# Hybrid encoder on one core: the low part of the far weight pages from a GpSimd subtraction instead of a negated copy and an accumulating DMA

## The chip, the core and the metric

The kernel runs on one core of a Trainium2 chip. The metric is the device time of one execution in microseconds; the kernel before takes 2670.23 us, the median of three runs (2668.58 to 2670.87). A core has TensorE (matmuls; PE in the profile, its weight loads PEld), VectorE (DVE), ScalarE (ACT), GpSimd (POOL) and SyncE (SP, which here only issues DMAs). Each engine works through its own queue in order; between engines only semaphores order the work. DMAs are issued from the queues of SyncE and GpSimd.

## What is computed

Two layers of a hybrid encoder on 256 tokens of width 4096, all in float32:

```python
h = rmsnorm(x, norm_w[l])
proj = h @ w_in[l]                       # 4096 x 11264
aq, ak, av, ag, rq, rk, rv, rg = jnp.split(proj, SPLIT_POINTS, axis=-1)
...                                      # rotary, grouped-query attention,
...                                      # bidirectional retention, gates
x = x + jnp.concatenate([a_out, r_out], axis=-1) @ w_out[l]   # 4096 x 4096
```

A final RMS norm follows. Nearly all of the work is the two products with `w_in` and `w_out`.

## The kernel before

**Three matmuls for one product.** TensorE multiplies in a float32 format with a shorter mantissa (fp32r). To keep float32 accuracy, each operand is split into a high part, rounded to fp32r, and a low part, the rest: `lo = x - hi`. A product is then three matmuls, hi·hi, lo·hi and hi·lo of weights and activations (lines 824 to 826). So every page of weights, 128 x 1024 float32 (512 KB), must be split on the core before TensorE can use it.

**How the weights are tiled.** A column block of 1024 outputs is worked through in 16 pairs of 256 rows, in four groups of four pairs. In the first pair of a group (`SEVEN`) a seven-product scheme in the manner of Strassen replaces eight products; it needs four pages (A, B and the sums T and U of raw pages, tiles `wsum`). Every other pair has two pages, A and B. There are 30 column blocks (11 for `w_in` and 4 for `w_out` in each of two layers) and 1200 pages; 960 of them are loaded as raw pages.

**Near and far pages.** 1082 pages are near. SyncE loads the raw page into one of five buffers (`wraw`, line 392), ScalarE casts it to the high part (`whi`), and VectorE subtracts (`wlo<-wraw,whi`); both parts stand in rings of five. The next load is issued when the low part has been put in its queue, and on the chip it waits for a free raw buffer.

The other 118 pages are far (`is_far`: page B of the pairs 2, 6, 10 and 14, but for the first two groups of the whole program). They go another way, past VectorE: `far_parts` has ScalarE cast the raw page to `fhi`, and ScalarE then writes the negated high part to `flo`; a DMA issued by GpSimd adds the same page of weights from HBM onto `flo`. So the raw buffer is free after the first copy, and its next load is issued at once, in `self.load()` at the end of `far_parts`. There is one buffer each for `fhi` and `flo`, and a far page is begun as soon as the far page before it is used up; it is used some ten pages later.

**What sets the order.** The program is written in a fixed order by a planner in Python. `ve` and `ac` wrap VectorE and ScalarE and add up an assumed cost for every operation (`ve.until`, `ac.until`); `now` is TensorE's planned time. Between products, `tick` puts in steps of other work (attention, retention, splitting of activations) where `room` finds that the parts of the coming pages will still be ready. Work for GpSimd's queue that belongs to far pages is kept in `self.adds` with the time from which it may be put in, and `add` puts it in when that time comes, or `take` does at the latest when the page is used:

```python
while self.adds and (now_all or self.adds[0][0] <= now.t + 0.5):
    self.adds.pop(0)[1]()
```

GpSimd's queue also holds the DMAs that store and fetch intermediate tiles (`store`, line 782, `fetch`, line 787, and the keys and values, line 1138) and the power in `rsqrt` (line 346). SyncE's queue holds the raw pages and some small tables and gains (`tables`, lines 318 and 321).

Of the kernel before, what the change touches and what calls it, by code (L numbers as in the profile page):

```python
# [13 lines left out]
AF = mybir.ActivationFunctionType  # L14
ALU = mybir.AluOpType
# [197 lines left out]
def hybrid_encoder(  # L213
# [15 lines left out]
    nc = tc.nc  # L229
    now = Now()  # L230
    ve, ac = Clock(nc.vector, vector_cost, now), Clock(nc.scalar, scalar_cost, now)
# [15 lines left out]
    def t(pool, shape, tag, bufs=None, dt=F32):  # L247
        kw = {} if bufs is None else {"bufs": bufs}
        return pool.tile(shape, dt, tag=tag, name=tag, **kw)

    def f32(v):
        return v.bitcast(F32)
# [99 lines left out]
    class Weights:  # L352
# [58 lines left out]
        def far_parts(self, g, src):  # L411

            g.hi = t(wp, [P, 2, NB], "fhi", FAR, F32R)
            g.lo = t(wp, [P, 2, NB], "flo", FAR, F32R)
            ac.copy(g.hi, src)
            ac.activation(g.lo, f32(g.hi), AF.Copy, scale=-1.0)
            g.high_at, g.low_at = ac.until, ac.until + FAR_LANDING
            self.adds.append((ac.until, partial(nc.gpsimd.dma_start, g.lo, g.src[0], accum_op=ALU.add)))
            self.load()

        def begin(self, g):

# [1142 lines left out]
```

## Time and profile before

| What | Value |
|---|---|
| three runs | 2670.87, 2670.23, 2668.58 us |
| profiled execution, span from first to last instruction | 2664.7 us |
| mean granted TensorE clock | 0.996 |
| DMA | 670.25 MB, mean 252 GB/s |
| far pages: negated copies on ScalarE | 118, 1062 ns each |
| far pages: accumulating DMAs | 86 for `w_in`, 32 for `w_out` |

The profile gives the span of its execution alone; the runs' times lie some 5.5 us above it.

How to read its lines. A group line names the source line, the engine, the operation, the tile written and the tiles read with their shapes, the count, the total busy time in us, the mean of one in ns, and then the idle time of the engine just before these instructions with what ended most of it. All of VectorE's and ScalarE's instructions carry line 198, that of the recording wrapper, so they are told apart by their tiles. A line of waits has the waiting instruction, what ended the wait, the sum in us, how often, and the longest. A line of the timeline has the start, the duration, the instruction, and in brackets the idle time before it with its releaser. SPq is SyncE's queue: its instructions only issue DMAs.

### The profile page before, as it was taken

The numbers are of one execution on the slowest core, as the hardware profiler recorded it, in microseconds if no ns is written. First come the engines' busy times: TensorE is split into PE (matmuls) and PEld (weight loads), VectorE is DVE, ScalarE is ACT, GpSimd is POOL, SyncE is SP. The second block draws the span as 40 slices with busy tenths as digits, with TensorE's granted clock in tenths as the row PEclk, the third lists the DMA queues.
The fourth block names the chain that finished last, engine by engine and source line by source line (L and its number), as shares of the span: only waits on it lengthen the run. The fifth ranks groups of instructions, "written<-read, shape, count | busy, mean of one in ns | idle before, by whom it ended". The sixth has DMA issues, their size and how long they took to land.

```text
span 2664.7 us, 33863 instructions
## 1 busy us (share of the span) xinstructions
PE 2621.3 (98%) x11832; PEld 2177.8 (82%) x11832; DVE 2079.2 (78%) x2579; ACT 1724.6 (65%) x2426; POOL 336.7 (13%) x478
## 2 busy tenths in 40 slices
PE   7999999999999999999999999999999999999997
PEld 5878888888888888888888888888888888888886
DVE  8877887887778797776978777887887688976765
ACT  7757676666555677555876666676565566865554
POOL 0011211111101110110111111211100011000000
PEclk9999999999999999999999999999999999999999
DMA  7888988887777787888888888988877787778885
GB/s 253 287 258 249 291 252 275 260 261 246 222 233 230 240 261 218 259 264 262 297 245 261 257 277 256 290 251 277 256 225 229 227 250 238 244 222 257 246 251 184
DMA packets 197660, 670.25 MB, mean 252 GB/s; under 512 B 23792, under 2 KB 30448, under 8 KB 197488
## 3 DMA queue, kind: packets, MB, share of 16 engines
q1 hardware_dynamic: 148912, 523.35, 57.2%
q0 software_dynamic: 48576, 144.73, 23.6%
q8 instruction: 92, 1.51, 0.2%
q14 instruction: 80, 0.66, 0.1%
HBM read 623.95 MB, written 44.04 MB: 251 GB/s over the span
## 4 chain that ended last, share of the span: by engine, by line
PE 92%; DVE 3%; DMA 3%; issue 1%; ACT 1%; POOL 0%; SPq 0%; POOLq 0%; DVEq 0%; ACTq 0%
PE M L825 30%; PE M L824 30%; PE M L826 30%; DVE wlo L198 1%; PE ps L825 1%; PE ps L826 1%; PE ps L824 1%; DMA wraw<-in_w_in 1%; DMA ca<-in_x 0%; DMA flo<-in_w_out 0%; DMA flo<-in_w_in 0%; ACT whi L198 0%; DMA tables<-in_k_norm 0%; DVE cb L198 0%; DVE x8l L198 0%
## 5 line engine op out<-in xcount | busy, mean ns | idle before, releaser
L198 ACT CAST whi<-wraw 128x1024 fp32r<-128x1024 f32 x842 | 820.7, 990 | 564.3 <-PE M L826 471.8
L198 DVE TENSOR_TENSOR wlo<-wraw,whi 128x1024 fp32r<-128x1024 f32 x842 | 950.4, 1143 | 272.5 <-ACT whi L198 261.0
L824 PE MATMUL M<-whi,x8h 128*128 128x512 f32 x1806 | 704.5, 390 | 0.4 <-DVE ca L198 0.3
L825 PE MATMUL M<-wlo,x8h 128*128 128x512 f32 x1806 | 704.0, 390 | 0.2 <-DVE wlo L198 0.2
L826 PE MATMUL M<-whi,x8l 128*128 128x512 f32 x1806 | 703.3, 389 | 0.0
L824 PEld LDWEIGHTS M<-whi,x8h 128*128 128x128 f32 x1806 | 339.9, 188 | 71.5 <-DVE ca L198 1.6
L826 PEld LDWEIGHTS M<-whi,x8l 128*128 128x128 f32 x1806 | 339.5, 188 | 71.0
L825 PEld LDWEIGHTS M<-wlo,x8h 128*128 128x128 f32 x1806 | 339.8, 188 | 70.1 <-DVE wlo L198 0.6
L198 ACT CAST whi<-wsum 128x1024 fp32r<-128x1024 f32 x240 | 252.6, 1053 | 180.2 <-PE M L826 161.2
L198 DVE TENSOR_TENSOR wlo<-wsum,whi 128x1024 fp32r<-128x1024 f32 x240 | 292.6, 1219 | 98.0 <-ACT whi L198 97.6
L825 PE MATMUL M<-wlo,x7h 128*128 128x512 f32 x840 | 327.5, 390 | 7.0 <-DVE wlo L198 7.0
L826 PE MATMUL M<-whi,x7l 128*128 128x512 f32 x840 | 327.5, 390 | 6.3 <-DVE x7l L198 6.3
L824 PE MATMUL M<-whi,x7h 128*128 128x512 f32 x840 | 327.1, 389 | 0.2 <-ACT whi L198 0.2
L824 PE MATMUL M<-whi,x 128*128 128x512 f32 x602 | 235.4, 391 | 9.2 <-ACT whi L198 9.2
L825 PE MATMUL M<-wlo,x 128*128 128x512 f32 x602 | 235.4, 391 | 1.2 <-DVE wlo L198 1.2
L826 PE MATMUL M<-whi,x 128*128 128x512 f32 x602 | 234.9, 390 | 0.0
L467 POOL DMA_DIRECT2D flo<-in_w_in x86 | 77.4, 900 | 1104.3 <-ACT flo L198 966.5
L198 DVE TENSOR_TENSOR wsum<-wraw 128x1024 f32<-128x1024 f32 x120 | 146.5, 1221 | 67.5 <-DMA wraw<-in_w_out 44.0
L198 ACT CAST fhi<-wraw 128x1024 fp32r<-128x1024 f32 x118 | 124.3, 1053 | 112.4 <-PE M L826 106.4
L826 PEld LDWEIGHTS M<-whi,x7l 128*128 128x128 f32 x840 | 157.9, 188 | 39.9 <-DVE x7l L198 7.1
L825 PEld LDWEIGHTS M<-wlo,x7h 128*128 128x128 f32 x840 | 157.8, 188 | 39.8 <-DVE wlo L198 7.8
L824 PEld LDWEIGHTS M<-whi,x7h 128*128 128x128 f32 x840 | 157.7, 188 | 32.7 <-ACT whi L198 0.7
(219 smaller groups left out, 3137.4 us busy)
## 6 DMA issues: line engine op xcount, KB each, us to landing
wraw<-in_w_in SPq DMA_DIRECT2D x703, 512.0 KB, 4.9
wraw<-in_w_out SPq DMA_DIRECT2D x256, 512.0 KB, 5.0
flo<-in_w_in POOLq DMA_DIRECT2D x86, 512.0 KB, 7.3
flo<-in_w_out POOLq DMA_DIRECT2D x32, 512.0 KB, 7.9
full<-next_dram POOLq DMA_DIRECT2D x18, 512.0 KB, 6.8
p_dram<-room POOLq DMA_DIRECT2D x64, 128.0 KB, 5.4
pT<-p_dram POOLq DMA_DIRECT2D x16, 512.0 KB, 5.9
next_dram<-room POOLq DMA_DIRECT2D x40, 128.0 KB, 5.7
```

The source lines that it names most:

```text
L198: return call(out, *args, **kwargs)
L467: self.adds.pop(0)[1]()
L824: nc.tensor.matmul(out, a[0], b[0], start=start, stop=False)
L825: nc.tensor.matmul(out, a[0], b[1], start=False, stop=False)
L826: nc.tensor.matmul(out, a[1], b[0], start=False, stop=stop)
```

## The change

In `far_parts` the negated copy and the accumulating DMA are gone. GpSimd subtracts the high part from the raw page instead, and the load that refills the raw buffer is put in behind the subtraction, since that reads the raw page.

```diff
             ac.copy(g.hi, src)
-            ac.activation(g.lo, f32(g.hi), AF.Copy, scale=-1.0)
             g.high_at, g.low_at = ac.until, ac.until + FAR_LANDING
-            self.adds.append((ac.until, partial(nc.gpsimd.dma_start, g.lo, g.src[0], accum_op=ALU.add)))
-            self.load()
+
+            def low():
+                nc.gpsimd.tensor_tensor(g.lo, src, f32(g.hi), op=ALU.subtract)
+                self.load()
+
+            self.adds.append((ac.until, low))
```

`FAR_LANDING`, the planner's allowance of 12 us until a far page's low part is there, stays.

## The prediction

> **What bounds the kernel now.** I read the page first, for the busy shares and the chain that ended last, and then the waits of the matmul engine.
>
> ```profile
> PE 2621.3 (98%) x11832; PEld 2177.8 (82%) x11832; DVE 2079.2 (78%) x2579; ACT 1724.6 (65%) x2426; POOL 336.7 (13%) x478
> PE 92%; DVE 3%; DMA 3%; issue 1%; ACT 1%; POOL 0%; SPq 0%; POOLq 0%; DVEq 0%; ACTq 0%
> ...
> PE M L824 <- ACT whi L198: 9.4, 3, 8.9
> PE M L825 <- DVE wlo L198: 8.5, 5, 5.6
> PE M L826 <- DVE x7l L198: 6.3, 2, 5.0
> PE M L825 <- DMA flo<-in_w_out: 1.2, 1, 1.2
> PE M L825 <- DMA flo<-in_w_in: 0.4, 1, 0.4
> ```
>
> TensorE is busy for 2621.3 of 2664.7 us. Its waits by name sum to 25.8 us, 8.9 of them the wait for the first page. Only 1.6 us (1.2 + 0.4) are waits for the low parts that the change makes in another way. So little can be won; the question is what the change takes away from the cover that keeps TensorE fed. That cover is made of VectorE and of the five raw pages:
>
> ```profile
> L198 DVE TENSOR_TENSOR wlo<-wraw,whi 128x1024 fp32r<-128x1024 f32 x842 | 950.4, 1143 | 272.5 <-ACT whi L198 261.0
> L198 DVE TENSOR_TENSOR wlo<-wsum,whi 128x1024 fp32r<-128x1024 f32 x240 | 292.6, 1219 | 98.0 <-ACT whi L198 97.6
> L198 DVE TENSOR_TENSOR wsum<-wraw 128x1024 f32<-128x1024 f32 x120 | 146.5, 1221 | 67.5 <-DMA wraw<-in_w_out 44.0
> ...
> L198 DVE TENSOR_TENSOR wsum<-wsum,wraw 128x512 f32<-128x512 f32 x120 | 83.1, 692 | 4.2
> L198 DVE TENSOR_TENSOR wsum<-wraw,wsum 128x512 f32<-128x512 f32 x120 | 82.0, 683 | 0.0
> ...
> L198 ACT ACTIVATE flo<-fhi 128x1024 fp32r<-128x1024 f32 x118 | 125.3, 1062 | 3.7
> L198 ACT CAST fhi<-wraw 128x1024 fp32r<-128x1024 f32 x118 | 124.3, 1053 | 112.4 <-PE M L826 106.4
> ...
> wraw<-in_w_in SPq DMA_DIRECT2D x703, 512.0 KB, 4.9
> wraw<-in_w_out SPq DMA_DIRECT2D x256, 512.0 KB, 5.0
> flo<-in_w_in POOLq DMA_DIRECT2D x86, 512.0 KB, 7.3
> ...
> SPq L392 <- DVE wlo L198: 1806.5, 667, 8.7
> SPq L392 <- ACT fhi L198: 119.6, 90, 4.4
> ```
>
> The near pages are 842 + 240 = 1082, one in 2664.7 / 1082 = 2.46 us. With a ring of five, a freed buffer is needed again four pages later, 9.9 us; less a cast (1.05, as `fhi`) and a subtraction (1.22), the low part stands ready 7.6 us early when nothing queues. The raw pages are 959 whole loads, one in 2.78 us; five slots turn round in 13.9 us, of which 4.9 are the transfer and 2.3 cast and subtraction, so a slot has 6.7 us to spare. The loads are one in-order queue on SyncE and wait for a slot nearly always: 1806.5 us for the subtraction that frees one, 119.6 us for the copy of a far page.
>
> **The change part by part.** *Removed from ScalarE*: 118 negated copies of 1062 ns, 125.3 us. ScalarE is 65% busy, so this is worth nothing except in the start. *Removed from the DMA*: 118 accumulating transfers of 512 KB, and TensorE's 1.6 us of waiting for them. I count −1.6.
>
> *Added to GpSimd*: 118 subtractions of 128x1024, each with two SBUF inputs. No row shows one. The only GpSimd arithmetic is the small power:
>
> ```profile
> L346 POOL TENSOR_TENSOR rst<-rst,half x16: 696/710/1615, 673.2 to 2356.2; 128x2 f32<-128x2 f32 x16
> ...
> 679.47 1.61 POOL L346 TENSOR_TENSOR rst<-rst,half 128x2 f32<-128x2 f32 x1 [5.56 <-DVE rst L198]
> ...
> 679.30 1.23 DVE L198 TENSOR_TENSOR wsum<-wraw 128x1024 f32<-128x1024 f32 x1
> 680.62 2.36 DVE L198 TENSOR_TENSOR wlo<-wraw,whi 128x1024 fp32r<-128x1024 f32 x2
> ```
>
> Its rate per element says nothing of a subtraction. I bound the price below by VectorE's same subtraction, 1.22 us, and above by the route replaced, 7.3 us from issue to landing. It is nearest to VectorE's row, one arithmetic step on the same shape; I take twice that, 2.4 us, as an estimate, since its smallest step above, on two elements, already takes 0.71 us. The Trainium skill, "GPSIMD Engine Reference", section 3.1, measures 4497 ns for an add of 2048 elements; half of that, an estimate of 2.25 us, would leave the sum as it is but for some tenths.
>
> *What it does to VectorE*: the power at 679.47 took 1.61 us where the median is 0.71. VectorE's operation with two SBUF inputs ran until 680.53; from there to the end at 681.08 are 0.55 us. So GpSimd stood still while VectorE read two tiles. That the reverse holds too (VectorE waits while GpSimd reads) this trace can't show, since two elements are read at once; from below it is no block at all, from above the whole 2.4 us. I take it as mutual. The Trainium skill, "SBUF — State Buffer", section "Who interferes with whom", says the same of a VectorE operation with two SBUF inputs against a GpSimd operation that reads SBUF: whichever is first keeps the other out for its whole length. This trace agrees in the one direction (1.61 against 0.71 us); with no block the sum below would lose its first term.
>
> The five VectorE rows above sum to 1554.6 us, 58% of the span. So a subtraction of 2.4 us costs VectorE 2.4 x 0.58 = 1.4 us on average, 164 us in all, and brings it from 78% to 84%. On average the 7.6 us lead hides that. Not where VectorE is full:
>
> ```profile
> 933.00:999.00 66.00, 66.00 (x303) 55.07 (x303) 60.24 (x96) 52.04 (x88) 6.76 (x10) 1.00 0.84 261
> 1266.00:1332.00 66.00, 64.83 (x287) 53.35 (x286) 62.56 (x118) 53.22 (x92) 10.47 (x17) 1.00 0.90 298
> 1399.00:1466.00 67.00, 67.00 (x297) 55.47 (x296) 58.93 (x88) 45.21 (x66) 11.13 (x14) 1.00 0.88 262
> 2265.00:2332.00 67.00, 67.00 (x302) 55.31 (x301) 63.95 (x99) 53.67 (x84) 3.70 (x5) 1.00 0.79 244
> ```
>
> The columns are PE, PEld, DVE, ACT and POOL busy. 118 pages in 2664.7 us are 2.9 in such a stretch, 4.1 us of block. VectorE has 5.8, 3.4, 8.1 and 3.1 us idle. If all of that idle could be used, the excess is 0.7 + 1.0 = 1.7 us; if none in the three fullest, 3 x 4.1 = 12.3. I take the middle, **+7**.
>
> *In the start* VectorE is on the path:
>
> ```profile
> 35.02 1.06 ACT L198 ACTIVATE flo<-fhi 128x1024 fp32r<-128x1024 f32 x1
> ...
> 37.64 1.23 DVE L198 TENSOR_TENSOR wlo<-wraw,whi 128x1024 fp32r<-128x1024 f32 x1 [0.68 <-ACT whi L198]
> ```
>
> Without the 1.06 us copy the cast behind it comes earlier, and VectorE loses its 0.68 us of idle; the first subtraction falls there and blocks 1.4 to 2.4 us. Net **+1.2** (0.7 to 1.7).
>
> *The moved load*: the load that refills a far page's slot is now issued behind the subtraction and waits for it on SyncE; behind it wait all later loads, and through them ScalarE's casts. Mostly it waits 2.4 us plus at most one VectorE operation, 1.2, inside the 6.7 us of a slot. But GpSimd's queue is in order too:
>
> ```profile
> POOL flo L467 <- ACT flo L198: 1427.9, 99, 47.6
> ...
> 861.14 1.06 ACT L198 ACTIVATE flo<-fhi 128x1024 fp32r<-128x1024 f32 x1
> ...
> 131.37 1.48 POOL L1138 DMA_DIRECT2D kv_dram<-vl  x2 [5.45 <-DVE vl L198]
> 132.84 0.94 POOL L467 DMA_DIRECT2D flo<-in_w_in  x1
> ...
> 868.54 0.89 POOL L1032 DMA_DIRECT2D rkq<-rq_dram  x1 [5.87 <-DMA rq_dram<-cb]
> 869.42 0.94 POOL L467 DMA_DIRECT2D flo<-in_w_in  x1
> ...
> 2178.83 0.94 POOL L467 DMA_DIRECT2D flo<-in_w_in  x1
> ...
> 133.27 0.59 SPq L318 DMA_DIRECT2D tables<-in_consts  x1
> ...
> 142.48 0.29 DVE L198 TENSOR_TENSOR C<-tables 128x128 f32<-128x128 f32 x1 [9.61 <-DMA tables<-in_k_norm]
> ```
>
> 99 of 118 times GpSimd was free and waited for ScalarE alone. At 869.42, and in the second layer at 2178.83, the far page stood behind a fetch that waited for its store. Until now that cost nothing but the low part's lateness: the slot was free at 861.1. Now it is held until 869.42 + 2.4 = 871.8, 10.7 us longer; that is 4.0 us more than the 6.7 to spare, partly under the 7.6 us lead of finished pages: 0 to 4 at each place, I take 2, together +4. At 132.84 the far page stands behind the stores of `vl`; SyncE's load then waits until 135.2, and the tables behind it, now issued at 133.27, go out 2.0 us later. VectorE idles 9.61 us for them, and TensorE's longest wait for `wlo` (5.6) is the same place: +1.5 (0 to 2), some of it returned by the missing transfer. Together **+5.5** (0 to 10).
>
> ScalarE's planned time is 1.05 us shorter for each far page, so some tasks move by a page; I count that at nothing, hidden by the lead of 7.6 us.
>
> The sum: +7 + 1.2 + 5.5 − 1.6 = +12.1, a span of 2676.8. The runs' median of 2670.23 lies 5.5 us over the profiled span; with that, **2682**.
>
> **The rivals.** *A, the cover holds*: the subtraction costs about 1.22 us, or VectorE isn't kept out. The block is then 0.7 us a page and 2.1 in a stretch, under the smallest idle of 3.1. The start nets nothing, the tables' +1.5 and the −1.6 cancel: 2670. For it speaks the 7.6 us lead; against it the 1.61 us of the power.
>
> *B, faster*: the transfers that are gone make the others land sooner.
>
> ```profile
> DMA packets 197660, 670.25 MB, mean 252 GB/s; under 512 B 23792, under 2 KB 30448, under 8 KB 197488
> ...
> DMA to landing us min/median/max: 4.4/6.4/8.9
> ```
>
> 118 x 0.524 MB are 62 of 670 MB, 9%. The tables that TensorE waits for land in up to 8.9 us; at the least, 4.4, that wait shrinks by 4.5. With −1.6 and −0.7 in the start: −6.8, 2663. Against it: everything that VectorE loses. It decides where the block is under some 0.5 us a page.
>
> *C, much slower*: the subtraction takes 4.9 us, four times VectorE's. The block is 2.8 us a page, 8.2 in a stretch; over the four idles above that is 12.5 (2.4 + 4.8 + 0.1 + 5.1) to 4 x 8.2 = 33, say 23. The start gives 3.5. The two late places hold 13.2 − 6.7 = 6.5 too long, half of it each, 6.5, and the tables 4.5. Less 1.6: +36, 2706. At the upper bound of 7.3 us VectorE loses 118 x 0.58 x 7.3 = 500 us (97% busy), and each slot is held 1.8 us over its spare (7.3 + 1.2 − 6.7), 212 in all: near 2890.
>
> **How the numbers follow.** The forecast has 0.44, its own range 2675 to 2695; A 0.20; B 0.14; C 0.16; its far end 0.06. About 0.2% (5.3 us) is what a measurement can tell from no change. Faster is B, 0.14; within is A and the forecast's lower edge, 0.22; slower 0.64. The range runs from 2664 to 2722: out are the far end, the upper part of C and half of B.
>
> **What would show it.** The subtraction's own duration on GpSimd (2.4; 1.2 for A, 4.9 for C), told by its spacing from what follows. VectorE's same subtractions longer than 1.22 us, or idle between them, beside it: 164 us in all. TensorE's waits for `wlo` up, most of it in 933 to 999, 1266 to 1332 and 2265 to 2332; its waits for `flo` gone. SyncE waiting some 9 us for GpSimd at about 862 and 2171, and the tables' wait near 140 longer than 5.6. Wrong it is if VectorE's operations keep their lengths beside the subtraction, or if TensorE's busy time itself grows.

## The result, and the profile after

The changed kernel takes 2684.59 us, the median of three runs (2684.30 to 2685.30), against 2670.23 before: +14.4 us, a ratio of 1.0055 with a 95% interval of 1.0035 to 1.0074. It is slower. The span of its profiled execution is 2683.5 us (2664.7 before).

The page of the kernel after: busy time by engine, the DMA total, the chain that ended last by engine, then one group of part 5 and two DMA issues of part 6.

```profile
PE 2630.1 (98%) x11832; PEld 2178.4 (81%) x11832; DVE 2190.9 (82%) x2579; ACT 1599.3 (60%) x2308; POOL 556.8 (21%) x478
...
DMA packets 180666, 608.36 MB, mean 227 GB/s; under 512 B 21904, under 2 KB 28560, under 8 KB 180496
...
PE 88%; DVE 7%; issue 2%; DMA 2%; ACT 1%; POOL 0%; SPq 0%; DVEq 0%; POOLq 0%; ACTq 0%
...
L419 POOL TENSOR_TENSOR flo<-wraw,fhi 128x1024 fp32r<-128x1024 f32 x118 | 325.0, 2755 | 1425.2 <-ACT fhi L198 1425.0
...
wraw<-in_w_in SPq DMA_DIRECT2D x703, 512.0 KB, 4.3
wraw<-in_w_out SPq DMA_DIRECT2D x256, 512.0 KB, 4.2
```

VectorE has the same 2579 instructions as before and is busy 111.7 us longer (2190.9 against 2079.2). The chain that ended last passes from TensorE (92% before, now 88%) to VectorE (3%, now 7%). What the change saves is there too, and buys nothing: ScalarE 125.3 us less, 62 MB less from HBM, pages that land in 4.3 us for 4.9. GpSimd is busy for 21% of the span, and of its 1425.2 us of idle time before the subtractions 1425.0 end with ScalarE's copy, so it is not the bound.

Groups of the kernel after, shapes kept apart; before, the first of them had a mean of 1219 ns, and the second is shown below it as it was:

```profile
L198 DVE TENSOR_TENSOR wlo<-wsum,whi 128x1024 fp32r<-128x1024 f32 x240 | 315.7, 1315 | 93.2 <-ACT whi L198 93.2
...
L198 DVE TENSOR_TENSOR cb<-cb,M 128x512 f32<-128x512 f32 x61 | 41.3, 679 | 0.8 <-PE M L829 0.7
```

```profile
L198 DVE TENSOR_TENSOR cb<-cb,M 128x512 f32<-128x512 f32 x61 | 41.4, 680 | 0.8 <-PE M L826 0.7
```

An operation with two inputs in SBUF has become longer; one that reads `M`, TensorE's output in PSUM, has kept its length (679 ns, 680 before). One place in the timeline shows why. The kernel after, GpSimd first, then VectorE (start, duration in us):

```profile
1460.86 2.95 POOL L419 TENSOR_TENSOR flo<-wraw,fhi 128x1024 fp32r<-128x1024 f32 x1
...
1460.34 1.22 DVE L198 TENSOR_TENSOR wlo<-wraw,whi 128x1024 fp32r<-128x1024 f32 x1
1461.48 3.41 DVE L198 TENSOR_TENSOR wlo<-wsum,whi 128x1024 fp32r<-128x1024 f32 x1
1464.81 0.75 DVE L198 TENSOR_TENSOR rot<-ca,S 128x256 f32<-128x256 f32 x2
...
1464.94 0.50 PE L828 MATMUL M<-wlo,x7h 128*128 128x512 f32 x1 [0.32 <-DVE wlo L198]
```

GpSimd's subtraction, issued at 1460.86, is 2.95 us long instead of 2.39, the shortest of the 118: it stood still until VectorE's first operation ended. VectorE's second operation is 3.41 us instead of 1.22: it stood still until GpSimd ended at 1463.81. TensorE took up this page's low part 0.05 us after it was done, and had waited 0.32 us. The same page before:

```profile
1446.00 1.22 DVE L198 TENSOR_TENSOR wlo<-wsum,whi 128x1024 fp32r<-128x1024 f32 x1
...
1450.48 0.39 PE L824 MATMUL M<-whi,x7h 128*128 128x512 f32 x1
```

It was done at 1447.22, and the matmul that reads it, the next after the one at 1450.48, came 3.49 us later. I call this time the lead of a page.

The waits of the kernel after, by engine: TensorE, SyncE, VectorE.

```profile
PE M L828 <- DVE wlo L198: 11.6, 16, 3.8
PE M L827 <- ACT whi L198: 10.9, 3, 9.8
PE M L829 <- DVE x7l L198: 7.6, 2, 7.1
PE M L827 <- DVE cb L198: 4.8, 3, 3.5
...
SPq L392 <- DVE wlo L198: 1532.3, 659, 8.9
SPq L392 <- POOL flo L419: 396.2, 109, 7.1
...
DVE C L198 <- DMA tables<-in_k_norm: 15.0, 2, 8.8
```

The waits for `flo` are gone; those for VectorE's tiles have grown from 15.1 us (8.5 + 6.3 + 0.3) to 25.0 (11.6 + 7.6 + 4.8 and 1.0 for `ca`). To see where TensorE loses time, slowed matmuls included, I set the start of each of its 11832 matmuls beside that of the matmul of the same number before. (In after 186 of them work on other tiles, since the planner moved some steps.) The table has how many us later it is, at some places given in the time of before. The kernels of experiments 9 (six blocks only), 11 (on VectorE) and 12 (VectorE, mixed) below stand beside it.

| at, us | after | six blocks only | on VectorE | VectorE, mixed |
|---|---|---|---|---|
| 9 (first matmul) | 0.95 | 0.11 | 0.06 | -0.16 |
| 60 | 2.88 | 1.71 | 1.49 | 1.40 |
| 150 | 2.16 | 3.91 | -1.62 | -0.73 |
| 933 | 2.41 | 3.44 | -2.31 | -1.41 |
| 1010 | 4.13 | 5.44 | -1.23 | -1.45 |
| 1332 | 6.14 | 7.95 | -2.17 | 1.17 |
| 1350 | 10.96 | 12.75 | 1.43 | 1.06 |
| 1466 | 16.17 | 17.27 | 2.47 | 1.06 |
| 2265 | 17.40 | 17.33 | 2.47 | 1.05 |
| end | 18.80 | 19.40 | 3.57 | 1.02 |

The span's 18.8 us are all here: 0.95 of a later first matmul (the first far page is copied at 35 us only, so this is no work of the change), 1.9 in the start, and 15.1 in five full stretches (1.7 from 933 to 1010, 2.0 from 1266 to 1332, 4.8 up to 1350, 5.2 up to 1466, 1.4 from 2265 on); the rest, 0.8, is small pieces of both signs. In the profiled runs whose time is known the run is 1.7 to 1.9 us longer than the span, so the profiled execution of before took about 2666.5 us, less than its three runs of 2668.58 to 2670.87; that is why the spans differ by more than the medians.

So a piece of one or two us in this table need not come of the change. The kernel of experiment 10 has no subtraction in these stretches and takes as long as before; by the same count it is 1.2 us later at 60 us and loses 1.8 from 1266 to 1350. The 10.0 us that after loses from 1332 to 1466 stand well above that (0.7 in that kernel).

### The profile page after: what moved, and what is told of

It reads as the page before. It is cut to its first block, busy times and chain, and to the rows that moved or that the text cites. A ratio compares the mean times of both kernels' runs of the same rounds, so it can differ in the third digit from the quotient of the medians.

```text
span 2683.5 us, 33629 instructions
## 1 busy us (share of the span) xinstructions
PE 2630.1 (98%) x11832; PEld 2178.4 (81%) x11832; DVE 2190.9 (82%) x2579; ACT 1599.3 (60%) x2308; POOL 556.8 (21%) x478
## 4 chain that ended last, share of the span: by engine, by line
PE 88%; DVE 7%; issue 2%; DMA 2%; ACT 1%; POOL 0%; SPq 0%; DVEq 0%; POOLq 0%; ACTq 0%
PE M L827 28%; PE M L828 28%; PE M L829 28%; DVE wlo L198 3%; PE ps L827 1%; PE ps L828 1%; PE ps L829 1%; DVE x8l L198 1%; DVE wsum L198 1%; DMA wraw<-in_w_in 1%; DMA tables<-in_k_norm 0%; ACT whi L198 0%; DVE cb L198 0%; DVE x L198 0%; DMA ca<-in_x 0%
## 5 line engine op out<-in xcount | busy, mean ns | idle before, releaser
L419 POOL TENSOR_TENSOR flo<-wraw,fhi 128x1024 fp32r<-128x1024 f32 x118 | 325.0, 2755 | 1425.2 <-ACT fhi L198 1425.0
L198 DVE TENSOR_TENSOR wlo<-wsum,whi 128x1024 fp32r<-128x1024 f32 x240 | 315.7, 1315 | 93.2 <-ACT whi L198 93.2
```

The costliest lines, as they stand in the source:

```text
L198: return call(out, *args, **kwargs)
L419: nc.gpsimd.tensor_tensor(g.lo, src, f32(g.hi), op=ALU.subtract)
```

## The experiments

Each kernel was timed in five rounds beside the kernel before, and the loss given is against that. Theory P is the prediction's: VectorE, kept out by GpSimd's subtraction where it is full, is the larger part. Its main rival was that the moved load and GpSimd's in-order queue are; others are told in the expectations.

**1. The block alone.** The kernel before, its loads issued early as they were, with a GpSimd operation ahead of the accumulating DMA (the copy's scale of −0.5 makes up for the doubling).

```diff
-            ac.activation(g.lo, f32(g.hi), AF.Copy, scale=-1.0)
+            ac.activation(g.lo, f32(g.hi), AF.Copy, scale=-0.5)
...
-            self.adds.append((ac.until, partial(nc.gpsimd.dma_start, g.lo, g.src[0], accum_op=ALU.add)))
+            def low():
+                nc.gpsimd.tensor_tensor(g.lo, f32(g.lo), f32(g.lo), op=ALU.add)
+                nc.gpsimd.dma_start(g.lo, g.src[0], accum_op=ALU.add)
+            self.adds.append((ac.until, low))
             self.load()
```

> The kernel before (negated copy, accumulating DMA, early refill of the raw slot), with one more GpSimd operation per far page: flo = flo + flo on 128x1024 ahead of the DMA, the copy's scale being -0.5. It reads two SBUF tiles on GpSimd as long as the subtraction does, but holds no raw page. Theory P (VectorE is kept out while GpSimd reads): VectorE's busy time rises by about 100 us as in the changed kernel, 2680 to 2690 us. Theory H (the raw slot's later release costs the time): 2668 to 2673 us, SyncE not waiting for GpSimd.

Measured: 2683.18 against 2669.92 us, +13.3 (1.0045, 1.0033 to 1.0058). The page of this kernel:

```profile
PE 2631.1 (98%) x11832; PEld 2182.7 (81%) x11832; DVE 2172.3 (81%) x2579; ACT 1724.3 (64%) x2426; POOL 585.8 (22%) x596
...
L420 POOL TENSOR_TENSOR flo<-flo 128x1024 fp32r<-128x1024 f32 x118 | 242.8, 2058 | 1450.4 <-ACT flo L198 1414.1
```

No load waits for GpSimd here, and nearly the whole loss is there. The GpSimd operation beside VectorE is enough. It reads one tile as both inputs, so it is somewhat shorter than the subtraction (a mean of 2058 ns for 2755).

**2. The hold alone.** The kernel before with a tiny GpSimd operation that reads the raw page and the load behind it; a power of 128x11 was to give it the length of the subtraction without reading much.

```diff
+    two, held_by = t(cp, [P, 11], "two"), t(cp, [P, 11], "held_by")
+    nc.gpsimd.memset(two, 2.0)
...
-            self.adds.append((ac.until, partial(nc.gpsimd.dma_start, g.lo, g.src[0], accum_op=ALU.add)))
-            self.load()
+            def low():
+                nc.gpsimd.tensor_tensor(held_by, two, f32(g.hi)[:, 0, :11], op=ALU.pow)
+                nc.gpsimd.tensor_tensor(held_by, held_by, src[:, 0, :11], op=ALU.subtract)
+                nc.gpsimd.dma_start(g.lo, g.src[0], accum_op=ALU.add)
+                self.load()
+            self.adds.append((ac.until, low))
```

> The kernel before, with two small GpSimd operations per far page (a power and a subtraction on 128x11, the second reading the raw page) ahead of the accumulating DMA, and the refill of the raw slot issued behind them. The raw page is held about 2.8 us longer by GpSimd, as in the changed kernel, but GpSimd reads only 11 elements at a time. Theory P: VectorE's busy time stays within 15 us of 2079, 2667 to 2674 us. Theory H: SyncE waits some 400 us for GpSimd and the time is 2680 to 2688 us.

Measured: 2696.03 against 2669.92 us, +26.1 (1.0095, 1.0079 to 1.0112), as neither expected. TensorE's waits in this kernel:

```profile
PE M L833 <- DVE wlo L198: 14.1, 7, 9.7
...
PE M L833 <- DMA flo<-in_w_in: 6.0, 2, 3.2
PE M L833 <- DMA flo<-in_w_out: 2.0, 1, 2.0
```

The edit did more than hold the load: the accumulating DMA went out behind two GpSimd operations, and TensorE waited 8.0 us for it where before it waited 1.6. The tables near 140 us also went out 6.2 us later, and the wait of 9.7 us for `wlo` is there. So this run doesn't tell the hold from late transfers; what the rest of its loss comes of stays open. The next experiment separates them.

**3. The hold, clean.** The accumulating DMA is issued first, then one GpSimd operation on 128x8 elements that reads the raw page, then the load.

```diff
+    held_by = t(cp, [P, 8], "held_by")
...
-            self.adds.append((ac.until, partial(nc.gpsimd.dma_start, g.lo, g.src[0], accum_op=ALU.add)))
-            self.load()
+            def low():
+                nc.gpsimd.dma_start(g.lo, g.src[0], accum_op=ALU.add)
+                nc.gpsimd.tensor_tensor(held_by, src[:, 0, :8], f32(g.hi)[:, 0, :8], op=ALU.subtract)
+                self.load()
+            self.adds.append((ac.until, low))
```

> The kernel before with one tiny GpSimd subtraction (128x8) that reads the raw page behind the accumulating DMA's issue, and the refill of the raw slot behind that. The slot is released about 1.06 + 0.3 + 0.9 + 0.45 = 2.7 us after the high part's copy, as in the changed kernel, without a long GpSimd read and without the transfer being issued later (which the earlier hold-only run did: TensorE waited 8.0 us for flo there). If the later refill costs by itself: 2676 to 2684 us. If the block of VectorE is all of it: 2668 to 2673 us, except for the tables, whose issue on SyncE is put off (up to +4).

Measured: 2672.92 against 2670.02 us, +2.9 (1.0012, 1.0003 to 1.0021). The waits of SyncE in this kernel show that the loads were held:

```profile
SPq L393 <- POOL held_by L422: 246.7, 109, 4.1
```

This hold is shorter than the change's (246.7 us of waits for 396.2) and costs 2.9 us. It is a small part; after the 13.3 us of experiment 1 little is left for it in any case.

**4. ScalarE's copy kept.** After, with the negated copy still made, which GpSimd adds to the raw page.

```diff
             ac.copy(g.hi, src)
+            ac.activation(g.lo, f32(g.hi), AF.Copy, scale=-1.0)
...
-                nc.gpsimd.tensor_tensor(g.lo, src, f32(g.hi), op=ALU.subtract)
+                nc.gpsimd.tensor_tensor(g.lo, src, f32(g.lo), op=ALU.add)
```

> The changed kernel with the negated copy on ScalarE put back; GpSimd adds the raw page to it instead of subtracting. ScalarE's 125 us return, all else stays. If what is left of ScalarE's work is worth nothing (P and H alike): 2683 to 2687 us. If the saved copies had paid back part of the loss: 2688 us or more. The copy puts the GpSimd operation 1.06 us later, so a shift of up to 2 us either way means nothing.

Measured: 2685.05 against 2669.92 us, +15.1 (1.0049, 1.0036 to 1.0062), as after. The 125.3 us that ScalarE is spared are worth nothing that these runs can tell.

This kernel also settles another question. Since the planner counts ScalarE's copy, leaving it out moves some steps, and after's program has another order than that of before. Here the order is that of before in all 11832 matmuls and 2579 VectorE instructions, and the loss is the same; so it isn't the new order. But it lies in other places: by the count of the table above, 5.8 us from 933 to 1010, 7.2 from 1266 to 1350, only 0.8 from 1350 to 1466, and 4.4 from 2265 to 2332.

**5. The subtraction twice.** After, with the GpSimd instruction repeated.

```diff
                 nc.gpsimd.tensor_tensor(g.lo, src, f32(g.hi), op=ALU.subtract)
+                nc.gpsimd.tensor_tensor(g.lo, src, f32(g.hi), op=ALU.subtract)
```

> The changed kernel with the subtraction done twice in a row for each far page. GpSimd then reads for 4.8 us. Theory P: VectorE's busy time rises by about another 110 us (2300), and since the full stretches already overflow, the time rises more than in proportion: 2705 to 2760 us. Theory H: the slot is held 2.4 us longer, 6.2 of its 6.7 us to spare: 2688 to 2700 us, with VectorE's extra busy time mattering little.

Measured: 2818.31 against 2669.92 us, +148.4 (1.0570, 1.0544 to 1.0597), more than either expected. Counting each VectorE operation that is over 0.1 us longer than the median of the same operation before, VectorE is stretched by 123.7 us in after and by 350 us here. 2.8 times the stretch makes ten times the loss: most of the first 124 us is covered, while 227 us more make 134 us more loss. The loads are held longer here too (SyncE waits 558.3 us for the second subtraction, 396.2 in after), and this run doesn't tell the two apart. By the same count the stretch is 101 us in experiment 1, 138 in experiment 4, and none at all in experiments 2 and 3.

**6. Cut in two.** After, with the subtraction as two instructions of 128x512.

```diff
-                nc.gpsimd.tensor_tensor(g.lo, src, f32(g.hi), op=ALU.subtract)
+                for k in range(2):
+                    nc.gpsimd.tensor_tensor(g.lo[:, k, :], src[:, k, :], f32(g.hi)[:, k, :], op=ALU.subtract)
```

> The changed kernel with each subtraction cut into two of 128x512. If GpSimd keeps the read port for the length of one instruction, VectorE gets in between the halves: the longest single block falls from about 2.4 to 1.3 us, GpSimd's time for a page rises to 3 us or more; 2676 to 2682 us. If the port isn't given up between the halves: 2683 to 2690 us with blocks as long as before.

Measured: 2679.14 against 2670.02 us, +9.1 (1.0031, 1.0019 to 1.0042). The instructions of the tile `flo` in this kernel (ns min/median/max, first and last start):

```profile
L420 POOL TENSOR_TENSOR flo<-wraw,fhi x236: 1271/1414/4247, 35.4 to 2635.8; 128x512 fp32r<-128x512 f32 x118
```

The same elements, 5.3 us less loss, although VectorE is stretched by 121.5 us in all, as in after. But now no VectorE operation is stretched by more than 1.24 us, except for three by 3.2 each. So VectorE gets in between the halves as a rule, and it matters how long one block lasts. The three are places where GpSimd had issued a DMA just ahead of the first half, and VectorE waited out both halves; why it did so there the rows don't show.

**7. The block planned.** After, with the planner told that each subtraction takes 1.05 us of VectorE, the mean stretch of after.

```diff
                 nc.gpsimd.tensor_tensor(g.lo, src, f32(g.hi), op=ALU.subtract)
+                ve.until = max(ve.until, now.t) + 1.05
```

> The changed kernel, with the planner told that VectorE loses 1.05 us at each subtraction (the mean block of the changed kernel's trace). VectorE's real work is the same. If the loss comes of steps that the planner puts in where VectorE has no room left: 2668 to 2678 us. If it comes of the block wherever it falls: 2681 to 2688 us.

Measured: 2705.24 against 2670.02 us, +35.2 (1.0129, 1.0115 to 1.0144); both expectations missed. TensorE's longest waits of it include a new one:

```profile
PE M L828 <- ACT x L198: 11.6, 2, 5.8
PE M L829 <- DVE wlo L198: 11.1, 11, 3.9
```

The planner now puts steps off, and TensorE waits twice for the activations that they make. This suggests that the planner's room is tight; where the loss of after comes from it doesn't show.

**8 and 9. Six column blocks.** Most of after's new waits lie in six of the 30 column blocks, which are counted from 0 through both layers and both matrices. One kernel has the route of before in these six (22 far pages) and the subtraction in the others (96 pages); the other kernel is its complement.

```diff
+                        blocks.append(b)
...
+                                one.full = len(blocks) - 1 in (0, 11, 14, 15, 16, 26)
...
+            if g.full:
+                ac.activation(g.lo, f32(g.hi), AF.Copy, scale=-1.0)
...
+            if g.full:
+                self.adds.append((ac.until, partial(nc.gpsimd.dma_start, g.lo, g.src[0], accum_op=ALU.add)))
+                self.load()
+            else:
+                self.adds.append((ac.until, low))
```

> The route is chosen by column block: the route before (negated copy, accumulating DMA) in blocks 0, 11, 14, 15, 16 and 26, in which the changed kernel's trace has its new waits, the GpSimd subtraction in the other 24. If the loss comes of the block of VectorE in its full stretches: 2665 to 2670 us, at or a little under the kernel before (the tables' wait and the waits for flo stay shorter). If it is spread over all pages: 2677 to 2682 us.

> The complement of the mixed kernel: the GpSimd subtraction only in the column blocks 0, 11, 14, 15, 16 and 26 (22 pages), the route of before in the other 96 pages. If the losses of stretches add up: 14.4 - 3.6 = 10.8 us over before, 2680 to 2682 us, with VectorE stretched by some 20 to 25 us in all. Rival (what the 22 cost, they cost only because the VectorE work put off by the other 96 reaches them): 2671 to 2675 us.

Measured: with the 96 pages 2673.65 against 2670.02 us, +3.6 (1.0009, 1.0000 to 1.0018), a little over its expected range, at the edge of what these runs can tell from before; with the 22 pages alone 2684.75 against 2669.71 us, +15.0 (1.0055, 1.0043 to 1.0068), all of after's loss and more than the sum expected. The 22-page kernel, its busy times:

```profile
PE 2628.7 (98%) x11832; PEld 2180.0 (81%) x11832; DVE 2114.2 (79%) x2579; ACT 1701.1 (63%) x2404; POOL 382.2 (14%) x478
```

VectorE is busy 35 us more than before, not 112, and the loss is the same. By shares of 118 pages the 22 would cost 2.7 us and the 96 would cost 11.7. So VectorE's total doesn't matter; what is taken from it in 22 places does. The two losses don't add up to that of after (3.6 + 15.0 against 14.4).

**10. Three other blocks.** The subtraction in blocks 1, 9 and 24 only (12 pages). The edit is against the first kernel of experiment 8.

```diff
-                                one.full = len(blocks) - 1 in (0, 11, 14, 15, 16, 26)
+                                one.full = len(blocks) - 1 not in (1, 9, 24)
```

> The GpSimd subtraction only in the column blocks 1, 9 and 24 (the waits of before for the tables near 140 us, and for a landed low part near 878 us, lie in the first two; the full stretches of the second matrix lie elsewhere), the route of before in all other blocks. If the loss sits in the full blocks (the run with six blocks on the old route says so): no loss, and the gain of the shorter wait for the tables (5.8 to 4.0 us) and of the wait for a landed part (0.5 us) stays: 2667 to 2670 us, a little under before. Rival (every GpSimd subtraction costs its share, 14.4 us over 118): 12 subtractions cost 1.5 us, 2671 to 2672 us.

Measured: 2668.91 against 2669.71 us (0.9998, 0.9989 to 1.0007): no difference. In these blocks the subtraction costs nothing that these runs can tell, and its small gains can't be told from nothing either. The interval reaches from 2.9 us under before to 1.9 over it, so the rival's 1.5 us is not excluded by this time; experiments 8 and 9 speak against it.

**11. The same subtraction on VectorE.** After, with VectorE doing the 118 subtractions, 144 us of work of its own.

```diff
-            def low():
-                nc.gpsimd.tensor_tensor(g.lo, src, f32(g.hi), op=ALU.subtract)
-                self.load()
-            self.adds.append((ac.until, low))
+            nc.vector.tensor_sub(g.lo, src, f32(g.hi))
+            self.load()
```

> After, with the low part's subtraction on VectorE in place of GpSimd, issued at the head of the page's load (behind the ScalarE copy of its high part), and the load of the next page right behind it; the copy's pass on ScalarE stays away. VectorE then does 118 subtractions of 1.22 us, 144 us of its own work, for the 112 to 124 us that the block of the GpSimd subtractions took from it, but it waits at each for a ScalarE copy that may be late, with its whole queue behind it. Theory P (the loss of after is VectorE time in the full stretches, little else): about the loss of after or 1.2 times it, 2683 to 2692 us, with TensorE's new waits for wlo again in the blocks near 1001, 1340 and 1400 to 1470 us; waits of VectorE for the copy add to it. Rival (VectorE time isn't the point, but GpSimd's in-order queue with the loads and tables in it): at or under before, 2664 to 2671 us, since GpSimd holds nothing any more.

Measured: 2670.15 against 2669.71 us (0.9998, 0.9989 to 1.0007): no loss that can be told, and theory P as I had written it is wrong by 13 to 22 us. The time is in the rival's range, but its reason falls with experiment 1, where no load waits for GpSimd. The busy times of this kernel, the tile `flo`, TensorE's waits for VectorE, and SyncE's for the subtractions:

```profile
PE 2625.0 (98%) x11832; PEld 2179.7 (82%) x11832; DVE 2206.3 (83%) x2697; ACT 1601.4 (60%) x2308; POOL 231.3 (9%) x360
...
L417 DVE TENSOR_TENSOR flo<-wraw,fhi x118: 1180/1219/1226, 35.8 to 2625.5; 128x1024 fp32r<-128x1024 f32 x118
...
PE M L825 <- DVE x7l L198: 6.0, 2, 5.0
PE M L824 <- DVE wlo L198: 5.9, 8, 1.9
PE M L823 <- DVE cb L198: 3.1, 3, 2.4
...
SPq L392 <- DVE flo L417: 341.5, 116, 5.1
```

VectorE is busier than in after (2206.3 against 2190.9) and TensorE waits less. The refill stands behind the subtraction here too, and SyncE waits 341.5 us for it, nearly the 396.2 of after; so the moved load is still in this kernel, without a loss that shows. The place shown above, in this kernel:

```profile
1448.85 1.22 DVE L198 TENSOR_TENSOR wlo<-wsum,whi 128x1024 fp32r<-128x1024 f32 x1
1449.98 1.22 DVE L417 TENSOR_TENSOR flo<-wraw,fhi 128x1024 fp32r<-128x1024 f32 x1
...
1452.99 0.39 PE L824 MATMUL M<-wlo,x7h 128*128 128x512 f32 x1
```

The page is done at 1450.07 and used at 1452.99: 2.92 us of lead are left of the 3.49, and in after none. The lead of some pages in the tight stretches, worked out in the same way (start of the first matmul that reads the low part less the end of the operation that made it):

| use before, us | before | after | on VectorE |
|---|---|---|---|
| 963.8 | 2.69 | 2.06 | 2.12 |
| 1281.3 | 1.77 | 0.06 | 0.84 |
| 1284.7 | 0.79 | 0.06 | 0.26 |
| 1325.0 | 3.15 | 0.06 | 0.81 |
| 1392.2 | 0.52 | 0.06 | 0.06 |
| 1441.2 | 2.45 | 0.06 | 1.89 |
| 1450.7 | 3.49 | 0.06 | 2.92 |

0.06 us means that TensorE waited or was about to. Before, the lead falls to 0.5 to 3.5 us in these places. A block stretches VectorE by 2.14 us in the median of the 22 pages of the six blocks, and by up to 3.0; a subtraction of VectorE's own takes 1.22. The one empties the lead, the other mostly fits in. It still loses where the lead is thinnest (3.6 us between 1332 and 1350, by the first table), and gets 3.1 back by 150 us, where the wait for `wlo` near 140 us is 2.1 us, 5.6 before.

**12. VectorE outside the six blocks.** The subtraction on VectorE, and the route of before in the six. The edit is against the first kernel of experiment 8.

```diff
             else:
-                self.adds.append((ac.until, low))
+                nc.vector.tensor_sub(g.lo, src, f32(g.hi))
+                self.load()
```

> The low part subtracted on VectorE (1.22 us a page) in all column blocks but 0, 11, 14, 15, 16 and 26, and the route of before in these six. Reading so far: what counts is the lead of VectorE's low parts over TensorE in the full stretches (0.5 to 3 us at the tightest pages of before): a page's 1.22 us fits into it nearly everywhere, a GpSimd subtraction's 2 to 3 us does not. In the kernel with all low parts on VectorE TensorE's waits were 3.7 us shorter than before's near 140 us (2.1 for 5.8), and some 6 us longer in the six full blocks. With these six on the old route the gain stays and the loss goes: 2664 to 2668 us, 0.1 to 0.2% under before. Rival (the shorter wait near 140 us comes from block 0's pages, or is taken back later): 2669 to 2671 us, as before.

Measured: 2666.20 against 2668.50 us (0.9990, 0.9981 to 0.9999). The loss from 1332 us on is gone: its matmuls fall back no further. It loses 2.6 us ahead of that, between 1266 and 1332, in a block with the route of before, where TensorE waits for an accumulating DMA (1.2 us before):

```profile
PE M L833 <- DMA flo<-in_w_out: 2.1, 1, 2.1
```

The time is in the expected range, but the gain is at the edge of what these runs can tell, and in its trace the last matmul is 1.0 us later than in that of before, not earlier. I don't call it faster.

## Why the prediction was right, and where its steps were wrong

The forecast was 2682 in 2664 to 2722, and 2684.6 was measured. Direction and mechanism were right: GpSimd and VectorE keep each other out, and TensorE then waits for VectorE. That the total came within 3 us is luck: the full stretches were put 8 us too low, the moved load with the tables 3 us or more too high, and part of what the traces show is the quick profiled run of before. The range was wide as well, 18 us below the forecast and 40 above.

- *The subtraction's duration*, taken as 2.4 us: 2.387 alone. Right, and with it the mutual block. That the block costs VectorE 0.58 of it, 1.4 us a page and 164 us in all, was somewhat high: 123.7 us, 1.05 a page. 53 of the 118 cost VectorE nothing: 21 fell beside no operation of VectorE, most others beside operations that read PSUM or beside a transposition with a single input.
- *The block in the full stretches, +7*: the mis-sized term. By the trace it is 15.1, twice as much (some 2 of it may be the difference between two runs), and 18.2 in that of experiment 4. I set the block of a stretch against the idle time that VectorE has in it. That measure put the loss into 933 to 999, 1266 to 1332 and 2265 to 2332, where 4.5 us are (1.1, 2.0 and 1.4), and called 1399 to 1466 safe, with 8.1 us idle, where 4.3 are; 4.8 more lie just behind the second stretch. In the kernel of experiment 4 the three have 9.8 us, and 1399 to 1466 has 0.8. So the same blocks in another order of steps fall on other tight pages, and idle time by stretch gives neither the size nor the place. What decides is the lead at the tightest page and the length of a single block, as experiments 6, 8, 9 and 11 show.
- *The start, +1.2*: 1.9, of which 1.2 stand in the kernel of experiment 10 too, with no subtraction there; so the term can't be told from nothing. TensorE's wait for `x7l` there is 7.1 us, not 5.0, and an operation on `x` that stands ahead of it in VectorE's queue is stretched to 2.71 us (its row is in the last section).
- *The moved load and the late places, +5.5*: too high. A hold alone, if a shorter one, costs 2.9 us (experiment 3), and one nearly as long as the change's goes with no loss in experiment 11. The late place in GpSimd's queue is there, as this timeline of after shows, and below it SyncE's waits for GpSimd between 850 and 890 us: at most 3.7 us, not 9 (4.1 near 2171). TensorE doesn't wait at all between 850 and 900.

```profile
871.07 0.89 POOL L1035 DMA_DIRECT2D rkq<-rq_dram  x1 [4.66 <-DMA rq_dram<-cb]
871.98 2.56 POOL L419 TENSOR_TENSOR flo<-wraw,fhi 128x1024 fp32r<-128x1024 f32 x1
```

```profile
SPq L392 <- POOL flo L419: 5.6, 2, 3.7
```

- *The tables*, +1.5 of these 5.5: they did go out later, and TensorE still waited less, 3.8 for 5.6 us. SyncE's queue and VectorE in after:

```profile
138.03 0.42 SPq L321 DMA_DIRECT2D tables<-in_k_norm  x1
...
143.55 0.29 DVE L198 TENSOR_TENSOR C<-tables 128x128 f32<-128x128 f32 x1 [8.80 <-DMA tables<-in_k_norm]
```

From issue to use are 5.5 us; before they were 8.6 (133.91, for this small table not shown there, to 142.48). The mechanism of rival B, faster landing, is real here, and it is what the term left out. It goes with the accumulating transfer that goes out at 132.84, just ahead of the tables. In the kernel of experiment 10, which lacks it in this block, issue to use are 5.3 us; in that of experiment 9, which has it there (135.19, table at 136.29), they are 8.9, and TensorE's wait is 6.6; in that of experiment 1, where the transfer goes out behind the tables (135.94, table at 135.05), 5.7. What it is worth in time is too little to tell: TensorE's wait is 4.7 us in experiment 10.
- *The waits for `flo`, −1.6*: gone, as said.
- *The baseline*: the 5.5 us between span and median, which I added, is no constant of an execution. 3.7 of it, by the 1.8 us between run and span, is that the profiled run was a quick one. Adding the predicted change of +12.1 to the median itself gives 2682.3, so it did no harm.

Rival A needed a block of 0.7 us a page; at 1.05 on average, and 2.14 in the median of the 22 pages that count, it does not hold. Rival C needed a subtraction of 4.9 us.

## What to carry to other kernels

Price work that blocks an engine by the longest single block against the smallest lead of what that engine delivers, place by place; here neither its busy share nor its idle time in windows of 66 us told the loss. A GpSimd operation that reads SBUF is not free work beside a VectorE that mostly has two SBUF inputs: 118 subtractions cost 14.4 us on GpSimd and nothing measurable as the same 118 on VectorE itself. If such an operation must go to GpSimd, cut it small, and keep it out of the stretches where the lead is thin.

## What the hardware showed that I had not expected

*A wait of TensorE can cost more than its length.* After a wait of 3.51 us in after, and of 2.42 in the kernel with the low part on VectorE, the matmuls go on at half clock for about 3 us. Windows of after (PE, PEld, DVE, ACT, POOL busy, granted clock, DMA share, GB/s):

```profile
1347.00:1350.80 3.80, 0.35 (x2) 0.00 (x0) 3.73 (x7) 0.64 (x2) 0.00 (x0) 1.00 0.37 113
1352.50:1355.20 2.70, 2.70 (x8) 2.14 (x7) 2.70 (x5) 0.41 (x1) 0.05 (x1) 0.50 0.16 26
1357.00:1361.00 4.00, 4.00 (x19) 3.31 (x18) 2.45 (x2) 2.02 (x3) 0.62 (x1) 1.00 0.84 239
```

At a clock of 0.50 a matmul starts every 0.43 us instead of 0.227. Of the timeline of the kernel on VectorE:

```profile
1341.46 0.80 PE L823 MATMUL M<-whi,x7h 128*128 128x512 f32 x1 [2.42 <-DVE cb L198]
...
1343.76 0.63 PE L825 MATMUL M<-whi,x 128*128 128x512 f32 x1
1344.89 0.40 PE L825 MATMUL M<-whi,x8l 128*128 128x512 f32 x1
```

So the wait of 2.42 us cost another 1.6 (0.36 and six times 0.20). The Trainium skill, "TensorE: Matmul & The Clock Gate", Part 1, has the clock fall to a half after an idle window of some 3.4 us; the half clock agrees, but here shorter waits were enough. A wait of 1.17 us was not: behind that of before at 1290 us, for `flo<-in_w_out`, the granted clock is 1.00.

*GpSimd can lose its turn several times over.* In the start of after, GpSimd and then VectorE:

```profile
36.07 5.60 POOL L419 TENSOR_TENSOR flo<-wraw,fhi 128x1024 fp32r<-128x1024 f32 x1 [35.62 <-ACT fhi L198]
...
35.63 1.22 DVE L198 TENSOR_TENSOR wsum<-wraw 128x1024 f32<-128x1024 f32 x1
36.77 2.35 DVE L198 TENSOR_TENSOR wlo<-wraw,whi 128x1024 fp32r<-128x1024 f32 x2
39.04 0.42 DVE L198 TENSOR_TENSOR x7l<-full,x7h 128x256 fp32r<-128x256 f32 x1
39.38 2.71 DVE L198 SCALAR_TENSOR_TENSOR x<-full,nw,x 128x128 fp32r<-128x128 f32 x2
```

Ready at 36.07, it got in only behind four operations of VectorE that follow each other without a gap, and then took its 2.39 us up to 41.67, for which the last one (before, two such were 0.60 us at 1335.70) waited. The Trainium skill, "SBUF — State Buffer", section "Who interferes with whom", has the port that the two engines share as an exclusive lock, for which a VectorE instruction with two SBUF inputs contends with a GpSimd instruction that reads SBUF. These rows agree with that. They also show that the one who waits need not get the next turn: three VectorE operations began while GpSimd waited.

The longest block of after, 3.0 us at 1281.4, fits less well: VectorE's operation on `xf`, of 0.28 us otherwise, began 0.73 us ahead of the subtraction's recorded start and still waited it out. GpSimd had been issuing a DMA meanwhile; the cause is not shown.
